# First loads of a two-layer trunk in a pool of their own, adaLN products in 256 columns, the dt projection beside B and C

## The chip, the cores and the metric

The kernel runs on one core of a Trainium2 chip (trn2). The metric is the device time of one execution in microseconds; runs of a kernel differ by about 0.2%.

## The reference, cut to what matters

Two layers over 512 latent tokens and 256 context tokens of width 1024, all in float32. Only the start of a layer matters here: the adaLN shift and scale of the two conditioning vectors, the modulated RMS norm, and the first columns of one combined projection, which feed the SSD scan.

```
shift, scale, gate = jnp.split(jax.nn.silu(c) @ w_ada + b_ada, 3, axis=-1)
...
h  = rms_norm(x) * (1.0 + scale[:, None]) + shift[:, None]
hc = rms_norm(xc) * (1.0 + scale_c) + shift_c
...
p = h @ w_in
xbc, dt_raw, k, v, u, uv, g_a, z, q, g_c = jnp.split(p, _cuts(CTX_SIZES + LAT_SIZES), axis=-1)
...
xh, bm, cm, dts = ssd_prepare(xbc, dt_raw, conv_w, conv_b, dt_bias)
ys, _, _ = ssd_bidir(xh, bm, cm, dts, a_neg, hf_c, hb_c, True)
```

`ssd_prepare` convolves the columns of x, B and C and turns `dt_raw` into step sizes; the scan needs cumulative sums of these.

## The kernel before, in words

Activations lie feature-major in SBUF: 8 feature blocks (k = 0 to 7) of 128 rows by 768 tokens, 256 of context first. Each product of float32 factors is made of three passes: every factor is split in a high part and a rest (`h_hi`, `h_lo`; `whi`, `wlo`), and high by high, rest by high and high by rest are accumulated in one PSUM bank. A bank holds 512 columns, so a projected block of 128 columns takes two banks, one of 512 columns (latents, `fl`) and one of 256 (context, `fcx`).

The order on each engine is made by a scheduler that simulates the program when it is built, and takes what is ready by priority (`tc.high_priority`); on the chip each engine runs its instructions in that order. Tiles with the same tag share a few buffers, and a writer waits for the last reader of its buffer.

Layer 0 begins in `first_layer_in`. The SP queue issues the loads: the conditioning vectors `cc`, the weights of B and C (`rawb`, `rawc`, 512 KB each), six token tiles `xn` of 512 KB (L257), then w_ada in 16 tiles `wa` of 128 columns (L265, 512 KB, rows of 512 bytes), which share four buffers with the tag `Fb`. ACT, POOL and DVE normalize the token tiles (Square L288, power L141 and L142, scaling L290). For each feature block k, `ada_in(k)` makes the shift and scale: 16 narrow products `pa` of 128 columns (L270), a copy `part` to SBUF by ACT (L272), two products with `sel` that sum the four partial rows (L274), and `mod` by DVE (L275). It is called two blocks ahead (`NAH = 2`). Then the normalized tiles are transposed by PE into `pt` (L297), DVE applies `mod` while reading the bank (`hf`, L299), ACT makes `h_hi` (L145), DVE makes `h_lo` (L146), and PE multiplies the block into the four open banks of B and C, three passes each (L305 to L307).

The dt projection, 32 columns as a two-part weight `wst`, is written behind it as two accumulations of 16 products (`accdt`, L496 to L499), copied to `dtf` by ACT (L500). Then come the convolutions (ACT copies the banks to `xp`, L450 and L451, DVE adds the taps, L456) and the next projected blocks (`proj`, the products `accc`, L387, L391, L392). A block's weights need one of two buffers `whi`: ACT writes it (`whic`, L145), then DVE its rest (`wloc`, L146). From `dtf` a chain of small steps leads to cumulative sums, which POOL writes to memory (`csd`, L551) and reads back spread over the partitions (`Fb`, L601); DVE and ACT make the scan's decay factors of it (L605, L608).

```
def ada_in(k):
    with tc.high_priority((HPW0, HPW1, HPW)[min(k, 2)] if FL else HPW):
        wa = [sp.tile([P, KD, P], F32, tag="Fb", bufs=4, name=f"wa0_{k}_{i}") for i in range(2)]
...
for k in range(NAH):
    ada_in(k)
```

Of the kernel before, what the change touches and what calls it, by code (L numbers as in the profile page):

```python
# [11 lines left out]
F32 = mybir.dt.float32  # L12
F32R = mybir.dt.float32r
# [31 lines left out]
NAH = 2  # L45
HPX = 20000
HPS = 20000
HPW = 9000
# [5 lines left out]
DTB = "sc"  # L54
TKD = -1
FL = 0
HPW0 = 50000
HPW1 = 14000
HPC = 12000
# [3 lines left out]
LAG = 1  # L63
# [28 lines left out]
def tile_hybrid_trunk(ctx: ExitStack, tc: tile.TileContext, ins, out: bass.AP):  # L92
# [59 lines left out]
    def params(li):  # L152
# [3 lines left out]
        with tc.high_priority(0 if li or not FL else 8 * HP):  # L156
            nc.sync.dma_start(prm, ins["prm"][li])
        L.b_ada = prm[:, 0:24]
# [27 lines left out]
    def ada_steps(mp, todo):  # L186
        """todo: (layer, its index, first of four blocks); one step for each block"""
# [63 lines left out]
    def first_layer_in(L, sp, sx, ws, w_split):  # L251
        """norm and modulation of the inputs by feature blocks, the first projections beside it"""
        xn = [sx.tile([P, 3, DM], F32, tag="xT", bufs=2, name=f"xn{i}") for i in range(2)]
        rs = small.tile([P, TT, 2], F32, tag="rs0", bufs=1, name="rs0")
        for t in (2, 3, 4, 5, 0, 1) if FL else range(TT):
            with tc.high_priority(HPC if FL and t < 2 else HPX):
                nc.sync.dma_start(xn[t // 3][:, t % 3, :], x_rows(0, t))  # L257

        def ada_in(k):
            """shift and scale of feature block k"""  # L260
            with tc.high_priority((HPW0, HPW1, HPW)[min(k, 2)] if FL else HPW):
                wa = [sp.tile([P, KD, P], F32, tag="Fb", bufs=4, name=f"wa0_{k}_{i}") for i in range(2)]
                for i in range(2):
                    c0 = DM * i + P * k
                    nc.sync.dma_start(wa[i], ins["w_ada"][0, :, c0 : c0 + P].rearrange("(k p) m -> p k m", p=P))  # L265
            pa = bank("sc", f"pa0_{k}")
            for i in range(2):
                for q in range(KD):
                    j = q % 4
                    pe.matmul(pa[32 * j : 32 * j + 32, P * i : P * i + P], sc[:, q, :], wa[i][:, q, :], start=q < 4, stop=q >= 4)  # L270
            part = small.tile([P, 2, P], F32, tag="part0", name=f"part0_{k}")
            act.activation(part, pa[:, 0:256].rearrange("p (i m) -> p i m", i=2), AF.Copy)  # L272
            for i in range(2):
                pe.matmul(pa[:, 256 + 2 * i : 258 + 2 * i], part[:, i, :], sel, start=True, stop=True)  # L274
                dve.tensor_scalar(  # L275
                    L.mod[:, 8 * i + k, :], pa[:, 256 + 2 * i : 258 + 2 * i], L.b_ada[:, 8 * i + k : 8 * i + k + 1], float(i), ALU.add, ALU.add
                )

        lat = [bank("acc", f"fl{i}") for i in range(2)]
        cx = [bank("sc", f"fcx{i}") for i in range(2)]  # L280
        for k in range(NAH):
            ada_in(k)
        with tc.high_priority(HPS):
            hl = [w_split(c0, name) for c0, name in ws]
        if not FL:
            for t in range(TT):
                xt = xn[t // 3][:, t % 3, :]
                act.activation(h_lo[:, 6:8, 0:512], xt.rearrange("p (a b) -> p a b", a=2), AF.Square, accum_out=rs[:, t, 0:1])  # L288
                rstd_pow(rs[:, t, 1:2], rs[:, t, 0:1], 1.0 / DM, EPS)
                dve.tensor_scalar(xt, xt, rs[:, t, 1:2], None, ALU.mult)  # L290
            for k in range(KD):
                hf32 = t3(f"hf0_{k}")
                for s, (o, n) in enumerate(SEGS):
                    pt = bank("at", f"pt0_{k}_{s}")
                    for i in range(n // P):
                        t = o // P + i
                        pe.transpose(pt[:, P * i : P * i + P], xn[t // 3][:, t % 3, P * k : P * k + P], ident)  # L297
# [5 lines left out]
                for i, (hi, lo) in enumerate(hl):  # L303
                    for acc, sl in ((cx[i][:, :NCX], slice(0, NCX)), (lat[i], slice(NCX, NT))):
                        pe.matmul(acc, hi[:, k, :], h_hi[:, k, sl], start=k == 0, stop=False)  # L305
                        pe.matmul(acc, hi[:, k, :], h_lo[:, k, sl], start=False, stop=False)
                        pe.matmul(acc, lo[:, k, :], h_hi[:, k, sl], start=False, stop=k == KD - 1)  # L307
        else:
# [819 lines left out]
```

## Time and profile before

| what | value |
|---|---|
| time, median of 3 runs | 1448.0 us (1446.86 to 1449.85) |
| profiled execution, first to last instruction | 1448.3 us |
| PE busy | 1337.9 us, 92% |
| DVE busy | 945.3 us, 65% |
| ACT busy | 656.1 us, 45% |
| POOL busy | 214.5 us, 15% |
| mean granted TensorE clock | 0.964 |

The profile gives the profiled execution as its span; no other time of that execution is listed beside it, and it lies within the three runs. PE is busy in nearly the whole span, so what matters is where it stands idle and where it runs at less than its full clock; both are read from tables of short stretches and from the engines' timelines. PE is TensorE, DVE VectorE, ACT ScalarE, POOL GpSimd, SP the queue of SyncE; L12 is line 12.

### The profile page before, as it was taken

Reading aid. Unit: us, or ns where it says so; the run is one execution under the profiler, and the core shown is the slowest. Engines: PE = TensorE matmul, PEld = TensorE weight load, DVE = VectorE, ACT = ScalarE, POOL = GpSimd, SP = SyncE. Lnnn points to the kernel's source line nnn. Section 1 sums busy time; section 2 is a strip of 40 time slices with the busy share of each in tenths; the row PEclk is TensorE's granted clock in tenths of the full one; section 3 lists DMA queues with packets and bytes.
Section 4 is the critical chain, followed back from the end, with each engine's and each line's share of the span. In section 5 each row is a group of like instructions: output and inputs, shape, how many; then the busy total and the mean of one; then the engine's idle time right before and its main releaser. Section 6 shows DMA issues by size and latency. Waiting matters only on the chain.

```text
span 1448.3 us, 21208 instructions
## 1 busy us (share of the span) xinstructions
PE 1337.9 (92%) x7944; PEld 1101.8 (76%) x7944; DVE 945.3 (65%) x1465; ACT 656.1 (45%) x1406; POOL 214.5 (15%) x418
## 2 busy tenths in 40 slices
PE   4999999999988999999999989999999689989987
PEld 3787888778867787788887768778778557778765
DVE  4497897587576657775232458887677477787432
ACT  3257634624455547554121235833623455575320
POOL 2002023113101113220000000202213001222000
PEclk8999999999999989999999999999999899989999
DMA  9424255745937447567878522625737954557885
GB/s 290 125 74 131 72 164 169 204 127 189 310 112 200 138 138 237 168 202 255 249 236 238 160 67 64 161 84 164 219 102 205 255 155 127 188 161 231 267 270 162
DMA packets 271782, 255.97 MB, mean 177 GB/s; under 512 B 14384, under 2 KB 223552, under 8 KB 271680
## 3 DMA queue, kind: packets, MB, share of 16 engines
q1 hardware_dynamic: 176624, 126.07, 31.1%
q0 software_dynamic: 18800, 66.68, 14.7%
q10 hardware_dynamic: 76256, 61.88, 13.9%
q8 instruction: 62, 1.02, 0.3%
q14 instruction: 40, 0.33, 0.1%
HBM read 199.12 MB, written 49.17 MB: 171 GB/s over the span
## 4 chain that ended last, share of the span: by engine, by line
PE 53%; DMA 18%; issue 12%; DVE 9%; ACT 6%; POOL 2%; SPq 1%; ACTq 0%; DVEq 0%; POOLq 0%
PE oacc L1027 4%; PE oacc L1026 4%; PE oacc L1025 4%; DMA Fb<-csd 3%; DMA yl<-ydr 3%; DMA qsq<-kq 2%; PE pS L585 2%; PE accc L387 2%; PE accc L391 2%; PE accc L392 2%; ACT Fb L608 2%; PE pO L790 2%; DMA qsk<-kq 2%; PE po L640 2%; PE acck L387 2%
## 5 line engine op out<-in xcount | busy, mean ns | idle before, releaser
L608 ACT ACTIVATE Fb<-Fb,dt_fp 128x128 f32<-128x128 f32 x320 | 98.6, 392 | 89.2 <-DVE Fb L605 89.2
L387 PE MATMUL accc<-h_hi,whic 128*128 128x512 f32 (+1 forms) x312 | 108.5, 348 | 5.5 <-ACT xp L451 3.8
L391 PE MATMUL accc<-h_lo,whic 128*128 128x512 f32 (+1 forms) x312 | 107.2, 344 | 0.0
L392 PE MATMUL accc<-h_hi,wloc 128*128 128x512 f32 (+1 forms) x312 | 106.8, 342 | 0.3 <-DVE wloc L146 0.3
L1025 PE MATMUL oacc<-wohi,yl 128*128 128x512 f32 x240 | 95.1, 396 | 5.0 <-DMA yl<-ydr 3.9
L1027 PE MATMUL oacc<-wohi,yl 128*128 128x512 f32 x240 | 95.4, 397 | 2.8 <-DMA yl<-ydr 2.8
L456 DVE SCALAR_TENSOR_TENSOR yv<-xp,hal,yv 128x772 f32<-128x772 f32 (+1 forms) x96 | 94.1, 993 | 5.7 <-ACT yv L454 4.5
L1026 PE MATMUL oacc<-wolo,yl 128*128 128x512 f32 x240 | 94.8, 395 | 1.0 <-DVE wolo L146 1.0
L756 ACT ACTIVATE Ea<-sm,mx 128x768 f32<-128x768 f32 (+1 forms) x80 | 65.2, 816 | 47.9 <-DVE mx L754 34.7
L605 DVE TENSOR_TENSOR Fb<-Fb,dt_cs 128x1024 f32<-128x1024 f32 x40 | 48.8, 1221 | 50.1 <-DMA Fb<-csd 50.0
L754 DVE TENSOR_REDUCE mx<-sm 128x1 f32<-128x768 f32 (+1 forms) x80 | 67.1, 843 | 13.6 <-PE sm L752 13.5
L387 PE MATMUL accz<-h_hi,whiz 128*128 128x512 f32 (+1 forms) x192 | 71.9, 375 | 0.8 <-DVE gtz L426 0.4
L391 PE MATMUL accz<-h_lo,whiz 128*128 128x512 f32 (+1 forms) x192 | 70.3, 366 | 0.0
L392 PE MATMUL accz<-h_hi,wloz 128*128 128x512 f32 (+1 forms) x192 | 70.1, 365 | 0.0
L387 PEld LDWEIGHTS accc<-h_hi,whic 128*128 128x128 f32 x312 | 59.4, 190 | 13.9 <-ACT xp L451 5.1
L749 PE MATMUL sm<-kh,qq 128*128 128x256 f32 (+1 forms) x144 | 52.5, 382 | 14.6 <-ACT Ea L756 12.9
L790 PE MATMUL pO<-v,wt 128*128 128x128 f32 x416 | 59.4, 295 | 6.5 <-DVE gg L801 4.8
L637 POOL DMA_DIRECT2D EF<-ecd x72 | 44.7, 627 | 139.3 <-DVE xT L642 128.3
L392 PEld LDWEIGHTS accc<-h_hi,wloc 128*128 128x128 f32 x312 | 59.5, 191 | 7.3 <-DVE wloc L146 0.5
L391 PEld LDWEIGHTS accc<-h_lo,whic 128*128 128x128 f32 x312 | 59.4, 190 | 6.8 <-issue 0.7
L790 PEld LDWEIGHTS pO<-v,wt 128*128 128x128 f32 x416 | 55.2, 207 | 11.6 <-DVE gg L801 5.5
L1043 DVE TENSOR_TENSOR go<-oacc,gate 128x512 f32<-128x512 f32 x20 | 13.7, 687 | 70.9 <-PE oacc L1027 70.9
(374 smaller groups left out, 3874.5 us busy)
## 6 DMA issues: line engine op xcount, KB each, us to landing
yl<-ydr ACTq DMA_DIRECT2D x120, 256.0 KB
wa<-in_w_ada SPq DMA_DIRECT2D x48, 512.0 KB
Fb<-csd POOLq DMA_DIRECT2D x40, 512.0 KB, 5.9
wo<-in_w_out SPq DMA_DIRECT2D x32, 512.0 KB
rawc<-in_w_in SPq DMA_DIRECT2D x22, 512.0 KB
EF<-ecd POOLq DMA_DIRECT2D x72, 128.0 KB, 3.1
rawz<-in_w_in SPq DMA_DIRECT2D x16, 512.0 KB
ydr<-yhi ACTq DMA_DIRECT2D x12, 384.0 KB
```

The costliest lines, as they stand in the source:

```text
L387: m = pe.matmul(acc[:, :n], hi[:, k, :], h_hi[:, k, o : o + n], start=k == 0, stop=False)
L391: pe.matmul(acc[:, :n], hi[:, k, :], h_lo[:, k, o : o + n], start=False, stop=False)
L392: pe.matmul(acc[:, :n], lo[:, k, :], h_hi[:, k, o : o + n], start=False, stop=k == KD - 1)
L456: dve.scalar_tensor_tensor(yv[:, lo_:], xp[:, lo_ + tap : tap + W2], L.convh[:, j, tap : tap + 1], yv[:, lo_:], ALU.mult, ALU.add)
L608: act.activation(Fb[:, h, :], Fb[:, h, :], AF.Exp, bias=fp[:, o : o + 1])
L749: m = pe.matmul(c_, H.qs[i][:, tsl], H.kh[i][:, k0 : k0 + kn], start=True, stop=False)
L754: dve.tensor_reduce(mx[:, i : i + 1], smap[:, s0 : s0 + nk], AX.X, ALU.min)
L756: act.activation(Es[i], smap[:, s0 : s0 + nk], AF.Exp, bias=mx[:, i : i + 1], scale=-1.0, accum_out=z[:, i, t % 2 : t % 2 + 1])
L790: pe.matmul(o_, H.w[:, k, P * ql : P * ql + P], H.v[:, k, :], start=k == 0, stop=k == nkt - 1)
L1025: pe.matmul(accs[t], yh[0][:, k, :], whi, start=q == 0 and k == 0, stop=False)
L1026: pe.matmul(accs[t], yh[0][:, k, :], wlo, start=False, stop=False)
L1027: pe.matmul(accs[t], yh[1][:, k, :], whi, start=False, stop=q == 3 and k == 3)
```

## The change

1. Layer 0's first loads go to a pool `start` that is open only while `first_layer_in` runs, and the scan's pools open after it in the same space. It holds the six token tiles and all of the shift and scale columns of w_ada, as eight tiles `wa` of 256 columns (1 MB each, rows of 1 KB). So no `wa` waits for a buffer. The token tiles are requested on the ACT queue, latents first; `wa` stays on SP; `prm` goes to the POOL queue.
2. `ada_in(q)` makes two feature blocks at once: 16 products of 256 columns (L277), one copy of 512 columns (L279), four products with `sel` into a second bank `pm` (L282), and two DVE operations for `mod` (L285). It is written just before the two blocks that need it. Banks of `pa`, `pm` and `pt` share the tag `at`, which has two buffers; `pa` had the tag `sc`.
3. The dt projection runs inside the loop over k: four more products for each k into two more banks of the tag `sc` (`fldt`, `fcdt`, L300 to L303). Its copies `dtf` are L324 and L325. Within a block the latents now come before the context.

The later program is written as before.

```diff
-        def ada_in(k):
-            with tc.high_priority((HPW0, HPW1, HPW)[min(k, 2)] if FL else HPW):
-                wa = [sp.tile([P, KD, P], F32, tag="Fb", bufs=4, name=f"wa0_{k}_{i}") for i in range(2)]
...
-            pa = bank("sc", f"pa0_{k}")
...
-        for k in range(NAH):
-            ada_in(k)
...
-                if k + NAH < KD:
-                    ada_in(k + NAH)
...
+        with tc.tile_pool(name="start", bufs=1, reuse_waits="tile") as su:
+            xn = [su.tile([P, DM], F32, name=f"xn{t}") for t in range(TT)]
...
+                    wa[q, i] = su.tile([P, KD, 256], F32, name=f"wa0_{q}_{i}")
+                    c0 = DM * i + 256 * q
+                    nc.sync.dma_start(wa[q, i], ins["w_ada"][0, :, c0 : c0 + 256].rearrange("(k p) m -> p k m", p=P))
+
+            with tc.high_priority(HPS0):
+                for t in (2, 3, 4, 5, 0, 1):
+                    nc.scalar.dma_start(xn[t], x_rows(0, t))
+                load_ada(0)
+                blocks, wst = weights()
+                for q in range(1, 4):
+                    load_ada(q)
...
+            def ada_in(q):
+
+                pa = bank("at", f"pa0_{q}")
+                for i in range(2):
+                    for k in range(KD):
+                        j = k % 4
+                        pe.matmul(pa[32 * j : 32 * j + 32, 256 * i : 256 * i + 256], sc[:, k, :], wa[q, i][:, k, :], start=k < 4, stop=k >= 4)
+                part = su.tile([P, 4, P], F32, tag="part0", bufs=2, name=f"part0_{q}")
+                act.activation(part, pa.rearrange("p (i m) -> p i m", m=P), AF.Copy)
+                pm = bank("at", f"pm0_{q}")
+                for i in range(4):
+                    pe.matmul(pm[:, 2 * i : 2 * i + 2], part[:, i, :], sel, start=True, stop=True)
...
+            ldt, cdt = bank("sc", "fldt"), bank("sc", "fcdt")
+
+            def dt_part(acc, k, sl):
+                if k == KD - 1:
+                    pe.matmul(acc[:32], wst[:, k, 0:32], h_lo[:, k, sl], start=False, stop=False)
+                pe.matmul(acc[:64], wst[:, k, :], h_hi[:, k, sl], start=k == 0, stop=k == KD - 1)
+                if k < KD - 1:
+                    pe.matmul(acc[:32], wst[:, k, 0:32], h_lo[:, k, sl], start=False, stop=False)
+
             for k in range(KD):
+                if k % 2 == 0:
+                    ada_in(k // 2)
...
+                for acc, adt, sl in ((lat, ldt, slice(NCX, NT)), (cx, cdt[:, :NCX], slice(0, NCX))):
...
+                    dt_part(adt, k, sl)
+            dtf = t3("dtf0")
+            act.activation(dtf[:64, NCX:], ldt[:64], AF.Copy)
+            act.activation(dtf[:64, :NCX], cdt[:64, :NCX], AF.Copy)
```

**Where the order changes: PE between two feature blocks.** Before, at the step from k = 4 to k = 5 (`pa_6` and `pa_5` are the adaLN products of feature blocks 6 and 5, `pt_5` the transposed block 5, `fl` and `fcx` the products of B and C):

```order
L307 MATMUL fl_150<-h_hi,wloc_0_216 128x512
L270 MATMUL pa_6_466<-wa_6_1_463,sc 32x128 x8
L297 MATMUL pt_5_0_504<-ident,xn_140 128x128 x2
L297 MATMUL pt_5_1_508<-ident,xn_140 128x128
L274 MATMUL pa_5_414<-sel,part_5_431 128x2
L305 MATMUL fcx_151<-h_hi,whib_0_209 128x256
L305 MATMUL fl_149<-h_hi,whib_0_209 128x512
```

Now, at the step from k = 1 to k = 2 (`pa_1` and `pm_1` belong to blocks 2 and 3, `pa_2` to blocks 4 and 5; four more rows of `pt` like those shown stand in the gap marked):

```order
L303 MATMUL fcdt<-h_lo,wst_134 32x256
L277 MATMUL pa_1_297<-wa_1_1_172,sc 32x256 x2
L282 MATMUL pm_1_316<-sel,part_1_314 128x2 x4
L313 MATMUL pt_2_1_324<-ident,xn_140 128x128
...
L313 MATMUL pt_2_0_330<-ident,xn_138 128x128
...
L313 MATMUL pt_3_1_353<-ident,xn_140 128x128
...
L319 MATMUL fl_207<-h_hi,whib_0_156 128x512
L319 MATMUL fl_208<-h_hi,whic_0_162 128x512
L301 MATMUL fldt<-h_hi,wst_134 64x512
...
L277 MATMUL pa_2_381<-wa_2_0_174,sc 32x256 x8
```

Before, the shift and scale of block 6 were in work while block 4 was multiplied, and what stood between two blocks had been prepared. Now 14 of the 16 adaLN products of a pair stand among the products of the pair before it, the last two directly ahead of it, and the sums `pm`, all twelve transposes of the pair and its first product stand behind them in one row. At the step from k = 3 to 4 it is the same with three products; at the step from 5 to 6 all 16 stand in block 4, and the row begins with `pm`.

**ACT at the end of the stage.** Before (`xp` are copies of the banks for the convolution, `whic` the high parts of the weights of the next two blocks, `dtf` the copy of dt):

```order
L145 ACTIVATE h_hi<-hf_7_580 128x768
L450 ACTIVATE xp_8_607<-fcx_151 128x256
L145 ACTIVATE whic_0_741<-rawc_0_739 128x1024
L451 ACTIVATE xp_8_607<-fl_149 128x512
L145 ACTIVATE whic_1_812<-rawc_1_810 128x1024
```

Now:

```order
L136 ACTIVATE h_hi<-hf_7_520 128x768
L324 ACTIVATE dtf_549<-fldt 64x512
L452 ACTIVATE xp_8_561<-fl_207 128x512
L136 ACTIVATE whic_0_653<-rawc_0_651 128x1024
L451 ACTIVATE xp_8_561<-fcx_209 128x256
L136 ACTIVATE whic_1_724<-rawc_1_722 128x1024
L325 ACTIVATE dtf_549<-fcdt 64x256
```

The weights of the next block, which stood behind one copy of 256 columns, stand behind two copies of 512. The copies of dt, which came after both convolutions' first steps, now come ahead of them or among them.

## Rows read from the trace of the kernel before

**Rows 1.** Stretches (us from the start): busy time of each engine (instructions), granted clock, DMA share, GB/s.

```profile
25.00:30.00 5.00, 3.83 (x13) 3.16 (x14) 3.92 (x17) 1.56 (x4) 0.00 (x0) 0.61 1.15 287
45.00:50.00 5.00, 5.00 (x30) 3.63 (x29) 1.39 (x3) 0.84 (x1) 0.00 (x0) 0.50 0.72 179
50.00:74.00 24.00, 23.95 (x216) 18.98 (x212) 12.05 (x21) 6.64 (x11) 0.34 (x6) 1.00 0.16 44
74.00:120.00 46.00, 45.73 (x271) 40.14 (x271) 41.78 (x66) 23.88 (x36) 0.68 (x12) 1.00 0.26 70
120.00:146.00 26.00, 23.31 (x145) 20.13 (x144) 18.70 (x21) 20.70 (x54) 9.51 (x21) 0.93 0.61 172
...
851.00:853.00 2.00, 0.36 (x3) 0.36 (x3) 2.00 (x7) 0.89 (x2) 0.17 (x3) 1.00 0.00 0
```

**Rows 2.** The same view, two stretches of the first loads.

```profile
7.50:12.50 5.00, 0.00 (x0) 0.00 (x0) 1.62 (x2) 1.57 (x2) 0.00 (x0) 1.00 1.03 405
...
20.00:45.00 25.00, 22.31 (x218) 15.85 (x211) 12.53 (x42) 5.42 (x13) 1.24 (x5) 0.76 1.20 283
```

**Rows 3.** Timeline of the SP queue: start, us, engine, line, operation, tiles, count.

```profile
6.08 11.42 SPq L265 DMA_DIRECT2D wa<-in_w_ada  x4
...
33.07 18.40 SPq L265 DMA_DIRECT2D wa<-in_w_ada  x8
```

**Rows 4.** Timeline of PE, first half of the stage; in brackets idle time and releaser.

```profile
19.47 1.08 PE L270 MATMUL pa<-wa,sc 128*32 128x128 f32 x16
...
27.81 0.77 PE L305 MATMUL fl<-h_hi,whib 128*128 128x512 f32 x1
...
42.73 0.67 PE L270 MATMUL pa<-wa,sc 128*32 128x128 f32 x16 [0.63 <-DMA wa<-in_w_ada]
...
48.09 0.63 PE L306 MATMUL fl<-h_lo,whic 128*128 128x512 f32 x1
48.51 0.63 PE L307 MATMUL fl<-h_hi,wloc 128*128 128x512 f32 x1
```

**Rows 5.** Timeline of PE, second half of the stage.

```profile
50.97 0.87 PE L297 MATMUL pt<-ident,xn 128*128 128x128 f32 x6
...
57.33 0.39 PE L306 MATMUL fl<-h_lo,whib 128*128 128x512 f32 x1
57.56 0.40 PE L307 MATMUL fl<-h_hi,wlob 128*128 128x512 f32 x1
```

**Rows 6.** Groups of instructions between 18 and 76 us: count, busy us, mean ns, idle before.

```profile
L145 ACT ACTIVATE h_hi<-hf 128x768 fp32r<-128x768 f32 x8 | 6.8, 845 | 18.2 <-DVE hf L299 18.2
L299 DVE TENSOR_SCALAR hf<-pt,mod 128x512 f32<-128x512 f32 x8 | 6.4, 803 | 0.5 <-PE pt L297 0.3
L274 PE MATMUL pa<-sel,part 128*128 128x2 f32 x32 | 5.6, 246 | 0.4 <-ACT part L272 0.4
L299 DVE TENSOR_SCALAR hf<-pt,mod 128x256 f32<-128x256 f32 x8 | 4.3, 541 | 0.2
...
L275 DVE TENSOR_SCALAR mod<-pa,prm 128x2 f32<-128x2 f32 x16 | 3.5, 217 | 18.7 <-PE pa L274 18.7
...
L146 DVE TENSOR_TENSOR wloc<-rawc,whic 128x1024 fp32r<-128x1024 f32 x2 | 2.5, 1226 | 3.4 <-ACT whic L145 3.4
```

**Rows 7.** Timeline of PE at the end of the stage.

```profile
73.42 0.28 PE L499 MATMUL accdt<-h_hi,wst 128*64 128x256 f32 x1
...
74.53 0.39 PE L392 MATMUL accc<-h_hi,wloc 128*128 128x256 f32 x1 [0.28 <-DVE wloc L146]
```

**Rows 8.** Timeline of ACT at the end of the stage.

```profile
72.17 1.05 ACT L145 ACTIVATE whic<-rawc 128x1024 fp32r<-128x1024 f32 x1
73.12 0.59 ACT L451 ACTIVATE xp<-fl 128x512 f32<-128x512 f32 x1
```

**Rows 9.** Timeline of PE where the scan's first factors are made.

```profile
134.46 0.50 PE L387 MATMUL accc<-h_hi,whic 128*128 128x512 f32 x1 [2.04 <-ACT xp L451]
```

**Rows 10.** Timeline of POOL in the same place.

```profile
122.72 3.57 POOL L601 DMA_DIRECT2D Fb<-csd  x4 [1.63 <-DMA csd<-cse]
```

More of the change, by code (lines that the diff above doesn't have):

```diff
@@ L44 @@
 NWP = 2
[L45 to L48, printed above, removed]
+HPS0 = 60000
 NPART = 2
@@ L62 @@
 HPV = 0
-LAG = 1
 NADA = (2, 1)
@@ L155, in params @@
         prm = small.tile([P, 24 + 12 * 6 + 21], F32, tag="prm", name=f"prm{li}")
-        with tc.high_priority(0 if li or not FL else 8 * HP):
+        if li:
             nc.sync.dma_start(prm, ins["prm"][li])
+        else:
+            with tc.high_priority(HPS0):
+                nc.gpsimd.dma_start(prm, ins["prm"][li])
         L.b_ada = prm[:, 0:24]
@@ L339, in first_layer_in @@
-        return [(cx[i][:, :NCX], lat[i]) for i in range(2)]
+                for acc, adt, sl in ((lat, ldt, slice(NCX, NT)), (cx, cdt[:, :NCX], slice(0, NCX))):
+                    for i, (hi, lo) in enumerate(blocks):
+                        pe.matmul(acc[i], hi[:, k, :], h_hi[:, k, sl], start=k == 0, stop=False)
+                        pe.matmul(acc[i], hi[:, k, :], h_lo[:, k, sl], start=False, stop=False)
+                        pe.matmul(acc[i], lo[:, k, :], h_hi[:, k, sl], start=False, stop=k == KD - 1)
+                    dt_part(adt, k, sl)
@@ L341, in tile_hybrid_trunk @@
+            dtf = t3("dtf0")
+            act.activation(dtf[:64, NCX:], ldt[:64], AF.Copy)
+            act.activation(dtf[:64, :NCX], cdt[:64, :NCX], AF.Copy)
+        return [(cx[i], lat[i]) for i in range(2)], dtf
     with tc.high_priority(HPR):
@@ L435, in finish, with dt_weights @@
             Q["yl"].dma_start(ydr[1, kt, :, tl0:], lo[:, tl0:].bitcast(F32))
-        with tc.tile_pool(name=f"ssd{li}", bufs=1, reuse_waits="tile") as sp, tc.tile_pool(name=f"ssx{li}", bufs=1, reuse_waits="tile") as sx, tc.tile_pool(name=f"ps_s{li}", bufs=3, space=PSUM, reuse_waits="tile") as ps2:
+        with ExitStack() as sstack:
+            ps2 = sstack.enter_context(tc.tile_pool(name=f"ps_s{li}", bufs=3, space=PSUM, reuse_waits="tile"))
+            def dt_weights(wst):
+                raw = load_w(C_DT, 32, f"dt{li}")
+                split(wst[:, :, 0:32], wst[:, :, 32:64], raw[:, :, 0:32])
+                return wst
+            if li == 0:
+                wst = gen.tile([P, KD, 64], F32R, name="wst0")
+                first, dtf = first_layer_in(
+                    L, bank, lambda: ([w_split(C_B, "b0_0"), w_split(C_C, "c0_0")], dt_weights(wst))
+                )
+            sp = sstack.enter_context(tc.tile_pool(name=f"ssd{li}", bufs=1, reuse_waits="tile"))
+            sx = sstack.enter_context(tc.tile_pool(name=f"ssx{li}", bufs=1, reuse_waits="tile"))
             W = TT * 32
@@ L481, in tile_hybrid_trunk @@
             if li == 0:
-                bc_blocks(0, first_layer_in(L, sp, sx, [(C_B, "b0_0"), (C_C, "c0_0")], w_split))
+                bc_blocks(0, first)
             else:
```

121 lines of the change are left out of this document (36 added, 85 removed).

## Prediction

> **What bounds the kernel now.** I read the table of short stretches first, because the page's shares (PE 92%) average over stages with different limits. The change touches one stage, from the first load to the end of the dt projection at 73.7 us [rows 7], so the question is what ends last there, and whether a delay gets through to the end afterwards. The stretches answer the second part: from 74 to 120 us PE is busy for 45.73 of 46 us at a granted clock of 1.00, with DVE at 41.78 [rows 1]. There is no slack that could swallow a shift, so what the stage loses or gains goes nearly one to one into the time, except where a later wait of PE becomes shorter.
>
> The stage has three parts. Up to 19.47 us loads bound it: the first adaLN product starts when its first tile is there, and the first product of B and C follows at 27.81 [rows 4], that is 8.3 us later. Then, to about 50 us, PE is busy but slow: the granted clock is 0.61 from 25 to 30 us and 0.50 from 45 to 50 [rows 1] (0.50 is the level of 1.2 GHz, 1.00 that of 2.4). The second fall came behind some microseconds of light work, adaLN products that used 32 columns of the array and an idle wait of 0.63 us for a load [rows 4]. Two products of 512 columns follow each other after 0.42 us there [rows 4] and after 0.23 us at the full level [rows 5]. From 50 us to the end PE is busy for 23.95 of 24 us at 1.00 [rows 1]: the two-block look-ahead keeps it fed.
>
> **The loads.** In the change 6.6 MB have to land before the first adaLN product can end: B and C 1.05, six token tiles 3.15, a pair of `wa` 2.1, and 0.25 of small ones. Token tiles (rows of 4 KB) moved at 405 GB/s, rows of 512 bytes at 283 [rows 2]. For rows of 1 KB nothing is shown; between the two I take 350. That gives 3.7 + 7.8 + 6.0 = 17.5 us; with the two rates put to `wa`, 16.7 to 18.9. The same sum for before, with half as much `wa` at 283, is 3.7 + 7.8 + 3.7 = 15.2 us against 19.47 measured, so 4.3 us are start and what shares the lines. Some of that sharing goes (the second pair comes behind the first), so I put the first adaLN products at 21.0, between 20 and 23. The Trainium skill (DMA: Bandwidth & Descriptors, Specifications) gives 512 B as the least transfer for line rate; by it 1 KB rows bring nothing over 512 B, and the sum would be 1.4 us longer. The trace disagrees as far as it goes, with 283 against 405 GB/s.
>
> That all loads are requested at once matters little after this. Before, the queue was held for 11.42 us over four `wa` and 18.40 over eight [rows 3], partly for buffers, but the lines were at 283 GB/s from 20 to 45 us anyway [rows 2]: 2.1 MB of a further pair need 6 to 7.4 us, and PE needs a pair only every 11 us. So I cost the three later pairs at nothing. The `prm` and `row` loads move too, and nothing early waits for them but `mod`, which comes after.
>
> From the first adaLN product to the first product of B and C I keep 8.3 us [rows 4]: the products are 16 of 256 columns (1.8 to 3.4 us by clock) for 32 of 128, and the copy, sum, `hf`, `h_hi` are the same steps in a row. First product of B and C: 29.3, 1.5 later than before.
>
> **The loop, at full clock.** For each k there are 12 products of B and C and 4 of dt, half of 512 columns (0.23 us [rows 5]) and half of 256 (half of it): 8 x 0.23 + 8 x 0.115 = 2.76 us, 5.5 for a pair. The dt products cost before what they cost now, only elsewhere. The adaLN products of a pair are 16 x 0.115 = 1.8 us, as before. What is new stands between the pairs. With no look-ahead for `pm`, and with two buffers for `pa`, `pm` and `pt`, this is a chain: copy `part` of 512 columns (0.59, as the ACT copy of 512 columns of a bank [rows 8]), four sums (0.5: 0.25 each by the group, two overlapping [rows 6]), two `mod` (2 x 0.22), `hf` (0.80 + 0.54), `h_hi` (0.85) [rows 6], and about 0.4 of hops: 4.1 us. In it PE does only the sums and twelve transposes, 12/6 x 0.87 = 1.7 us [rows 5]; it idles for about 1.9. Pairs start 5.5 + 1.8 + 4.1 = 11.4 us apart, the last of them 10.8, since there the copy is done ahead. Stage end: 29.3 + 11.4 + 11.4 + 10.8 + 5.5 = 68.4, 5.3 us earlier than 73.7. That gain is all from the slow clock before.
>
> **The clock.** I don't think it goes away. The first pair again starts behind light work; before, the first 8 us of B and C ran at the lower level, which cost about half of that. I take +3.5 (0 to +4.5). Then each of the three gaps has 4 us with sums and transposes alone and nearly 2 us of idle PE. For a fall: the light stretch ahead of 45 us, which was followed by 5 us at 0.50, at a cost of 2.5 or a little more [rows 1, 4]; and the wait of 2.04 us before 134.46 [rows 9], in a stretch whose clock is 0.93 [rows 1]. Against: from 851 to 853 us PE was busy for 0.36 of 2 us, and the clock in it stayed 1.00 [rows 1]. So each gap costs 0 to 3 us; I take 1.7, nearer to the fall because two cases speak for it, 5.1 in all. Stage end: 68.4 + 3.5 + 5.1 = 77.0, **+3.3**. With no fall 68.4 (-5.3), with all of them 81.9 (+8.2).
>
> **The hand-over.** Before, the next block's weights were being written while PE did the last dt products, and PE waited 0.28 us for `wloc` [rows 7]. Now dt ends with the rest, so those products no longer cover anything, and ACT does two copies of 512 columns (0.59 each) before `whic` (1.05 [rows 8]); behind it DVE makes `wloc` (1.23 [rows 6]). That is 3.5 us from the last use of B's weights, of which PE can fill about 0.6 with what is left of C and dt, and some with the passes that need no `wloc`. Taken: **+2.2** (1 to 3). Queued behind on ACT is the second `whic`, needed a block later: nothing.
>
> **Later.** With `dtf` copied first, the chain to `csd` starts earlier against the products, and the read of `Fb` at 122.72 [rows 10] with it. Of PE's 2.04 us at 134.46 and the lower clock around it (26 us at 0.93, about 1.8) [rows 1, 9] at most 3.8 can come back; I take **-1.5**. Later waits may be reshuffled a little; I give them no sign.
>
> **Sum.** +3.3 + 2.2 - 1.5 = +4.0 on the profiled execution's 1448.3, so 1452.3; that execution is 0.3 over the median of the runs, well inside their spread, so I round to 1452.5.
>
> **Rivals.**
> Faster: *PE keeps its full clock*. The loads come in one go, the first pair is dense (32 products and the adaLN of the next), and the gaps are short enough. Then the stage ends 5.3 us earlier, and -5.3 + 2.2 - 1.5 to -3.8 gives 1441.5 to 1443.7. For it: the 1.00 at 851 us. Against it: both falls in the stage before. It decides where the clock costs under 1.7 us in all four places together (under 4 if all of the late wait comes back).
> Unchanged: *gains and losses cancel*. The first pair is slow, the gaps are not: -5.3 + 3.5 + 2.2 - 1.5 = -1.1, 1447; one fall of 2.5 more makes 1449.7. It is the case between.
> Not what it says: *the loads aren't the limit that went*. If the first adaLN product waits for the whole 6.6 MB at 283 GB/s, the first pair starts 2 us later, and the later pairs still wait for nothing; 1454.5, inside my own case.
> Slower by more: every gap falls, +8.2 + 2.2 - 1.5 = +8.9, 1457; without the late gain 1459.
>
> **How the numbers follow.** My forecast with its slower neighbours (a fall at two or three gaps) has 0.52, and its own range is 1451 to 1460. The case between has 0.26 and the full clock 0.22. The range of 1442.5 to 1460 leaves out the ends of both sides. A difference of 0.2% (2.9 us) is about what can be told from no change: faster is under 1445.1, slower over 1450.9. The bounds fall between the cases, so the chances are 0.23, 0.25 and 0.52.
>
> **What would show it.** First product of B and C near 29 us; gaps of nearly 2 us of PE idle behind `pm`, each with a granted clock of 0.5 to 0.9 behind it; end of the stage near 77; the first `wloc` wait grown to 2 us; the wait before the first decay factors shorter than 2.04. The forecast is wrong if the clock stays at 1.00 from 30 us on, or if PE doesn't idle between pairs because the scheduler's order lets the transposes and `hf` of the second block cover it.

## The result, and the profile after

| | median | runs | ratio to before |
|---|---|---|---|
| changed | 1471.6 us | 1464.47 to 1477.69 (4) | 1.0158 [1.0120, 1.0196] |
| before, beside it | 1448.9 us | 1446.86 to 1452.98 (4) | |
| changed once more (e4) | 1469.5 us | 1462.33 to 1475.56 (6) | 1.0139 [1.0105, 1.0174] |

The change makes the kernel 20 to 23 us slower. I had forecast 1452.5 us and a range up to 1460: the sign was right, the size was not. The profiled execution has a span of 1475.9 us and took 1477.69 us, the most of the four, so what is read from its profile adds up to more than the medians lost.

PE's timeline of the changed kernel: the first products, the first gap between two pairs of blocks (in full) and the first product behind each of the other two, the hand-over to the next block (`accc`), and three later places. The rows answer to [rows 4, 5, 7, 9]:

```profile
20.15 1.94 PE L277 MATMUL pa<-wa,sc 128*32 128x256 f32 x16 [20.15 <-DVE sc L122]
...
30.12 0.80 PE L319 MATMUL fl<-h_hi,whib 128*128 128x512 f32 x1
30.71 0.63 PE L319 MATMUL fl<-h_hi,whic 128*128 128x512 f32 x1
31.14 0.56 PE L301 MATMUL fldt<-h_hi,wst 128*64 128x512 f32 x1
...
40.64 1.05 PE L282 MATMUL pm<-sel,part 128*128 128x2 f32 x8 [0.70 <-ACT part L279]
41.55 0.96 PE L313 MATMUL pt<-ident,xn 128*128 128x128 f32 x6
43.09 0.89 PE L313 MATMUL pt<-ident,xn 128*128 128x128 f32 x6 [0.58 <-DVE hf L315]
44.42 0.50 PE L319 MATMUL fl<-h_hi,whib 128*128 128x512 f32 x1 [0.44 <-ACT h_hi L136]
44.76 0.40 PE L319 MATMUL fl<-h_hi,whic 128*128 128x512 f32 x1
44.99 0.40 PE L301 MATMUL fldt<-h_hi,wst 128*64 128x512 f32 x1
...
57.45 0.50 PE L319 MATMUL fl<-h_hi,whib 128*128 128x512 f32 x1 [0.44 <-ACT h_hi L136]
...
68.89 0.50 PE L319 MATMUL fl<-h_hi,whib 128*128 128x512 f32 x1 [0.44 <-ACT h_hi L136]
...
74.98 0.28 PE L301 MATMUL fcdt<-h_hi,wst 128*64 128x256 f32 x1
76.73 0.38 PE L374 MATMUL accc<-h_hi,whic 128*128 128x256 f32 x1 [1.47 <-ACT whic L136]
...
77.99 0.39 PE L379 MATMUL accc<-h_hi,wloc 128*128 128x256 f32 x1 [0.76 <-DVE wloc L137]
...
143.03 0.50 PE L374 MATMUL accc<-h_hi,whic 128*128 128x512 f32 x1 [1.63 <-ACT xp L452]
...
397.65 1.54 PE L728 MATMUL pvt<-ident,vf 128*128 128x128 f32 x6 [3.55 <-DMA vf<-vd]
...
431.84 0.69 PE L776 MATMUL ptw<-ident,Ea 128*128 128x128 f32 x2 [5.49 <-DVE Ea L771]
```

The gap is there as forecast: PE waits for `part`, for `hf` and for `h_hi`, 1.72 us in all. The last dt product ends at 75.3 us, 1.6 later than [rows 7]. Then PE waits 2.23 us for the next block's weights, against 0.28 before. ACT's timeline shows why: the copy of dt and a copy of a bank come ahead of `whic` (before, [rows 8], `whic` was being made while PE did the dt products):

```profile
74.66 0.59 ACT L324 ACTIVATE dtf<-fldt 64x512 f32<-64x512 f32 x1 [4.26 <-PE fldt L301]
75.15 0.58 ACT L452 ACTIVATE xp<-fl 128x512 f32<-128x512 f32 x1
75.63 1.05 ACT L136 ACTIVATE whic<-rawc 128x1024 fp32r<-128x1024 f32 x1
```

The stretches, with the columns of [rows 1], show what follows that wait:

```profile
20.00:40.00 20.00, 18.53 (x116) 11.38 (x116) 8.02 (x15) 5.46 (x11) 3.94 (x8) 1.00 1.11 334
32.00:38.00 6.00, 6.00 (x48) 3.87 (x48) 1.03 (x2) 0.84 (x1) 0.00 (x0) 1.00 1.09 349
40.00:50.00 10.00, 8.35 (x65) 5.99 (x66) 6.85 (x26) 2.92 (x7) 0.17 (x3) 1.00 0.79 207
50.00:74.00 24.00, 20.96 (x150) 15.41 (x149) 9.15 (x16) 4.58 (x6) 0.34 (x6) 1.00 0.00 1
75.00:80.00 5.00, 2.77 (x19) 2.32 (x18) 3.29 (x3) 4.92 (x10) 0.00 (x0) 0.93 0.13 31
80.00:84.00 4.00, 4.00 (x19) 3.75 (x18) 3.96 (x6) 0.95 (x1) 0.00 (x0) 0.50 0.80 225
84.00:88.00 4.00, 4.00 (x12) 3.29 (x12) 4.00 (x9) 1.48 (x3) 0.17 (x3) 0.50 0.02 4
88.00:120.00 32.00, 32.00 (x183) 28.02 (x182) 25.11 (x44) 15.15 (x22) 0.51 (x9) 0.98 0.18 50
...
120.00:146.00 26.00, 23.63 (x142) 20.70 (x141) 21.14 (x24) 20.63 (x50) 7.92 (x17) 1.00 0.63 150
```

In this execution the clock stays at 1.00 through all three gaps and falls to 0.50 (the level of 1.2 GHz) from 80 to 88 us, behind the hand-over's wait: 8 us at half speed, 4 lost, and about 1 more by the rows on either side (0.93 and 0.98). So the scan's first blocks of products begin 7.6 to 9.8 us later than before, and the lag is still 10.4 us at the scan's end (367 us before). The rest comes later. The last two of PE's rows above lie in the first layer's attention, and behind the second stands this row of DVE's timeline:

```profile
430.36 0.69 DVE L688 TENSOR_TENSOR qsq<-qsq,sin 128x512 f32<-128x512 f32 x1 [4.16 <-DMA qsq<-kq]
```

Neither place was touched by the change, and before PE has neither wait. The lag against before is 19 us at the first MLP block (577.9 us before), 15 at the start of the second layer and 27.6 at the last output product. So three questions: what the start costs and which of its edits does it, why more is lost behind the scan, and how my sum stands to both.

### The profile page after: what moved, and what is told of

Same layout as the page of the kernel before. It is cut to its first block, busy times and chain, and to the rows that moved or that the text cites. A ratio compares the mean times of both kernels' runs of the same rounds, so it can differ in the third digit from the quotient of the medians.

```text
span 1475.9 us, 20899 instructions
## 1 busy us (share of the span) xinstructions
PE 1343.4 (91%) x7816; PEld 1103.5 (75%) x7816; DVE 942.9 (64%) x1457; ACT 657.2 (45%) x1402; POOL 217.3 (15%) x419
## 3 DMA queue, kind: packets, MB, share of 16 engines
q10 hardware_dynamic: 77120, 65.03, 14.3%
## 4 chain that ended last, share of the span: by engine, by line
PE 54%; DMA 22%; DVE 10%; issue 7%; ACT 5%; POOL 1%; ACTq 0%; SPq 0%; DVEq 0%; POOLq 0%
DMA Fb<-csd 4%; PE oacc L1026 3%; PE oacc L1024 3%; PE oacc L1025 3%; DMA qsq<-kq 3%; PE accc L374 2%; PE accc L378 2%; PE accc L379 2%; PE pO L789 2%; PE pS L584 2%; DMA yl<-ydr 2%; PE po L639 2%; DMA qsk<-kq 2%; DMA wo<-in_w_out 1%; PE accz L374 1%
## 5 line engine op out<-in xcount | busy, mean ns | idle before, releaser
L607 ACT ACTIVATE Fb<-Fb,dt_fp 128x128 f32<-128x128 f32 x320 | 98.7, 392 | 71.7 <-DVE Fb L604 71.7
L137 DVE TENSOR_TENSOR wolo<-wo,wohi 128x1024 fp32r<-128x1024 f32 x32 | 38.7, 1223 | 39.0 <-ACT wohi L136 39.0
```

The costliest lines, as they stand in the source:

```text
L607: act.activation(Fb[:, h, :], Fb[:, h, :], AF.Exp, bias=fp[:, o : o + 1])
```

## The experiments

In all of them the program computes the same as before. A ratio is against runs of the kernel before on the same chip; 0.1% is 1.4 us. The kernel before spread wider there than the 0.2% that I had started from: 1443.2 to 1453.6 us in eleven runs beside e1 to e4. Lags are starts of the same block of products, minus those of the profile before; the scan's first block is its first of 512 columns, at 77.26 us before.

That profile is one execution. All nine profiles that keep its later order (e1, e3, e5, e6, e9 and e12 to e15) gain 3 to 5 us on it between 475 and 600 us and lose 5 to 11 between 1150 and 1291 us, whatever their start. So a lag tells of a change as far as the scan's end; behind it the ratios count, and two profiles of the study against each other.

### The start, and the order of what comes later (e1, e2, e4)

The scheduler orders the whole program again when its start changes. Behind dt both kernels issue the same 10043 instructions, but 2660 of PE's 6534 stand in another place, and 651 of DVE's 1388. A table at the end of the kernel can hold those instructions to either order, by dependences that order two instructions on an engine and add no semaphore.

```diff
         tile_hybrid_trunk(tc, ins, out)
+        keep_order(tc)
...
+            if e in last:
+                tc.add_manual_dep(i, last[e].name, NOSYNC, reason="order of the table")
+            last[e] = i
```

e1 is the changed kernel with the later order of before, e2 the kernel before with the later order of the changed one, e4 the changed kernel as it is.

> The start of the changed kernel, and behind the dt projection the instructions of every engine in the order that they had in the kernel before (a table holds the order; nothing is computed otherwise). Theory L, most of the loss is in the later order that the scheduler made anew: only the start's part stays, the 7.6 to 10 us that separate the profiles from 85 to 390 us, so 1456 to 1459 and 1.005 to 1.007 of before. Theory S, the start alone costs it, and its delay makes the later transfers come at worse times: 1468 to 1474, ratio 1.013 to 1.018. In its profile the later waits of PE tell which: 3.5 us for vf and 5.5 us for Ea near 400 and 432 us should be gone by theory L.

> The start of the kernel before, and behind the dt projection the order of the changed kernel. Theory L: it loses what the later order costs, 10 to 14 us, 1459 to 1463. Theory S: the order costs nothing by itself, 1447 to 1451.

> The changed kernel itself, timed again on the same chip as the three others, since its four runs lie 13 us apart. Both theories: 1464 to 1478, median near 1471, ratio 1.012 to 1.019. If it comes out under 1460 the first result was partly chance.

Measured: e1 1.0100 [1.0066, 1.0133], e2 1.0094 [1.0058, 1.0131], e4 1.0139 [1.0105, 1.0174]. Both halves cost. On the old start the new order alone costs 14 us, well clear of the intervals; on the new start (e4 against e1) it is about 5.7, the size of the intervals. The two halves overlap. The profile of e4, the changed kernel's fastest run (1462.33 us), has a lag of 9.9 us at the scan's end and 12.3 at the end, where the first profile had 10.4 and 27.6. e1's lag is 8.6 us at the scan's first block and 7.8 at its end, with falls of the clock now at two of the three gaps, as I had forecast for each (44 to 48 and 58 to 62 us), and a smaller one behind the hand-over:

```profile
44.00:48.00 4.00, 3.37 (x14) 2.33 (x14) 3.45 (x7) 1.74 (x3) 0.00 (x0) 0.66 0.81 227
58.00:62.00 4.00, 3.43 (x14) 2.62 (x13) 3.09 (x5) 1.38 (x2) 0.00 (x0) 0.61 0.02 4
80.00:84.00 4.00, 2.70 (x16) 2.50 (x17) 3.44 (x4) 3.92 (x8) 0.00 (x0) 0.85 0.22 56
84.00:88.00 4.00, 4.00 (x19) 3.62 (x19) 4.00 (x5) 1.15 (x2) 0.00 (x0) 0.72 0.76 212
```

So which gap falls differs between executions: over six profiles of this start the stage ends at 75.3, 76.4, 77.4, 78.1, 78.4 and 79.1 us. Over four of the old start (before, e2, e7, e8) it ends at 73.7, 73.2, 71.7 and 71.4: the profile that every lag here is taken from is the latest of them.

### Which part of the order (e7, e8)

The old start, with the first layer's scan in the old order and the rest in the new one (e7), or the other way round (e8).

```diff
-    for text in (ORDER0, ):
+    for text in (ORDER0, ORDER1, ):
```

> The start of the kernel before; behind it the first layer's scan in the order of before, and from the attention of the first layer on the order of the changed kernel. The second run (all of the later order new) lost 14 us, of which its profile shows 9 in the scan. Theory L1, all of that loss is in the scan, where the dt chain was moved ahead: 1448 to 1452. Theory L2, the later parts cost as much as they seem to in the profile: 1454 to 1458.

> The counterpart: the start of the kernel before, the first layer's scan in the order of the changed kernel, the rest in the order of before. Theory L1: 1460 to 1464, PE waits 1.2 us for dtf near 78 us with a granted clock under 0.8 behind it. Theory L2: 1455 to 1459.

Measured: e7 1.0034 [1.0016, 1.0052], e8 1.0036 [1.0015, 1.0056]. No single place holds the loss. In e8's profile PE waits 1.19 us for the copy `dtf` at 75.97 and the clock is 0.84 and 0.82 in the next two stretches of 5 us; e7 has no such wait.

### The hand-over alone (e3)

e1, with the copies of dt behind the first steps of the convolutions and `whic` first on ACT.

```diff
-            act.activation(dtf[:64, NCX:], ldt[:64], AF.Copy)
-            act.activation(dtf[:64, :NCX], cdt[:64, :NCX], AF.Copy)
-        return [(cx[i], lat[i]) for i in range(2)], dtf
+        return [(cx[i], lat[i]) for i in range(2)], (ldt, cdt)
...
+                dtf = t3("dtf0")
+                act.activation(dtf[:64, NCX:], ldt[:64], AF.Copy)
+                act.activation(dtf[:64, :NCX], cdt[:64, :NCX], AF.Copy)
```

> The kernel of the first run of this study, with two changes at the end of the first stage: the copies of dt come after the first steps of both convolutions, and the next block's weights are the first thing that ACT does once B's weights are free. If the hand-over and the low clock behind it make up most of what the start lost, PE's idle time between the last dt product and the third product of the next block falls from 2.2 us to about 1.2, the granted clock of 79 to 86 us rises from about 0.5 to 1.00, and the time falls by 4 to 6 us against the first run. If the clock falls all the same: by 1 us only.

Measured: 1.0106 [1.0076, 1.0135], e1's ratio. The waits for `whic` and `wloc` fall from 1.47 and 0.76 us to 1.05 and 0.27, and the clock behind them holds, as PE's timeline and the stretches of e3 show:

```profile
79.15 0.39 PE L371 MATMUL accc<-h_hi,whic 128*128 128x256 f32 x1 [1.05 <-ACT xp L449]
...
79.92 0.39 PE L376 MATMUL accc<-h_hi,wloc 128*128 128x256 f32 x1 [0.27 <-DVE wloc L137]
```

```profile
80.00:84.00 4.00, 4.00 (x28) 3.78 (x29) 3.62 (x4) 3.91 (x8) 0.00 (x0) 1.00 0.69 180
84.00:88.00 4.00, 4.00 (x19) 3.19 (x17) 4.00 (x5) 0.81 (x2) 0.00 (x0) 1.00 0.30 88
```

The lag at the scan's first block falls to 5.4 us from 8.6, and the time does not move. In the two profiles e3's lag is below e1's up to 688 us (3.8 against 6.7), level with it at 866 (5.5 against 5.7) and above it from 942 on (8.7 against 6.4): what the hand-over gave is lost again, in these two at the change of layers and in the second layer's scan. Why it is lost, no run shows.

### The places of the scan's buffers (e5, e11)

The first tile with a tag decides where its buffers lie. Before, `wa` was the first `Fb`, and the scan's first tile; now `bT` comes first. In the changed kernel and in e1 the load `wsT` for the attention then lands in space that the scan still reads, and POOL holds it, and the queue behind it, for `py` (8.57 us in the changed kernel's profile). POOL's timeline of e1:

```profile
373.70 0.56 POOL L867 DMA_DIRECT2D wsT<-in_wsT  x1 [4.62 <-PE py L620]
```

e5 is e1 with two tiles that nothing uses, which put the buffers where they were. e11 does the same in the changed kernel, with the scheduler free.

```diff
+                sp.tile([P, 8, P], F32, tag="Fb", bufs=4, name="fb_first")
                 bc_blocks(0, first)
+                sp.tile([P, KD, 64], F32R, tag="H0", bufs=NHF, name="h0_first")
```

> The first run of this study (new start, later order of the kernel before), and the scan's pool gives its tiles the places that they had before: two tiles that nothing uses are allocated where the loads had stood, so that Fb lies at the pool's start again. In the first run POOL's loads for the attention (wsT) waited 4.6 us for a product that reads Fb, and PE waited 3.3 us for vf behind it, which it did not with the old start. Theory M, the shift of places is the cause: both waits fall under 1 us, and the time falls by 2 to 4 us against the first run, to 1459 to 1461. If the waits stay, the later burst of loads has another cause and the time stays near 1463.

> The changed kernel with two unused tiles at the head of the scan's pools, so that the scan's buffers lie where they did before; the scheduler is free. Theory 1, the places cost 3 to 5 us in the changed kernel as they did between e1 and e5: ratio 1.010 to 1.013, and the attention of the first layer without the 3 us wait for its load. Theory 2, the scheduler makes yet another order from the same edits and the places' gain is lost or doubled by it: a ratio outside 1.008 to 1.014, with the wait for the load gone all the same.

Measured: e5 1.0068 [1.0044, 1.0091], e11 1.0093 [1.0061, 1.0126]. POOL's timeline of e5 shows the load without a wait, and PE's the row that had waited 3.28 us in e1:

```profile
367.12 0.56 POOL L869 DMA_DIRECT2D wsT<-in_wsT  x1
```

```profile
390.03 0.87 PE L730 MATMUL pvt<-ident,vf 128*128 128x128 f32 x6 [0.23 <-DMA vf<-vd]
```

The places cost about 4.6 us (e1 against e5), and 6.7 in e11 against e4, where the order was made anew as well. The differences are of the size of the intervals, so the cost in time is likely and not shown; the wait itself is gone in both profiles.

### The loads and the 256 columns alone (e6, e9, e12)

e5 with dt behind B and C again and `pa`, `pm` in the banks `sc`, one pair ahead. (Four banks `sc` hold B's and C's context products and either dt or the look-ahead, so in these banks the one excludes the other; e14 below finds room for the look-ahead in `at`.)

```diff
-                pa = bank("at", f"pa0_{q}")
+                pa = bank("sc", f"pa0_{q}")
...
+            ada_in(0)
             for k in range(KD):
-                if k % 2 == 0:
-                    ada_in(k // 2)
...
+                if k % 2 == 0 and k < 6:
+                    ada_in(k // 2 + 1)
...
-                    dt_part(adt, k, sl)
```

> Of the change only the loads and the products of 256 columns: the adaLN products of a pair are called one pair ahead, in the banks that the dt products had taken, and dt is projected after B and C as before; places and later order are those of the run with the scan's map as before. Theory G, the lost look-ahead and the dt products in its place make the gaps, the hand-over wait and the low clock behind them: the first product of B and C starts at 29 to 30 us, no gap of over 0.7 us from there, the stage ends at 64 to 68 us (73.7 before, 75 to 79 changed), and the time is 1441 to 1446, faster than before. Theory K, the loads themselves make the start late or the clock falls whatever stands between the pairs: stage end 72 or later, and 1449 or more.

Measured: 0.9987 [0.9966, 1.0007], and letter for letter once more (e12) 0.9984 [0.9956, 1.0011].

> e6 once more, letter for letter. If the loads and the 256 columns alone are worth the 2 us that e6's ratio of 0.9987 suggests: 0.997 to 1.000 again, the stage at the start again ahead of the kernel before by 4 to 5 us. If e6 was luck: 1.000 to 1.003.

The loss of the changed start is gone. PE's timeline and a stretch of e6 show no gap up to the last dt product, which ends at 67.7 us, 6.0 ahead of [rows 7]; behind it PE waits 0.76 us for `wloc`.

```profile
33.16 0.48 PE L311 MATMUL fl<-h_hi,whib 128*128 128x512 f32 x1
...
67.38 0.28 PE L490 MATMUL accdt<-h_hi,wst 128*64 128x256 f32 x1
...
69.02 0.39 PE L367 MATMUL accc<-h_hi,wloc 128*128 128x256 f32 x1 [0.76 <-DVE wloc L137]
```

```profile
50.00:68.00 18.00, 17.90 (x116) 14.38 (x115) 7.41 (x15) 5.20 (x9) 0.17 (x3) 1.00 0.00 0
```

Of a lead of 5.5 us in the scan the medians keep about 2. e12's profile is ahead by 2 to 9 us until the second layer's attention and level from 1291 us on, where all these profiles lose against the one before; e6's is still 8.1 ahead at the end.

The first product of B and C came late there, at 33.16. ACT stands still for 5.08 us until `rawc` lands and can split it; behind it in its queue are four tiles' squares and the gate of `cc`. e9 orders these by hand ahead of it.

```diff
-HAND = ()
+HAND = (('I-183', 'I-93', 'I-187', 'I-191', 'I-195', 'I-199', 'I-203', 'I-164', 'I-229'),
...
```

(The first row is ACT's: the squares and, second, the gate's tanh, then C's split, I-164, and the first `part`.)

> The loads and the 256 columns alone, with dt behind B and C, as in e6, and with an order by hand on three engines: ScalarE squares all six input tiles and takes the gate's tanh ahead of C's weight split, VectorE follows it, and TensorE takes the first block's transposes ahead of the second pair's adaLN product; at the end of the stage the hand-over's first weight split comes first on ScalarE. In e6 the first projection began at 33.16 us and waited for the scaling of the input's tiles, while the stage ended at 67.7 us. Theory 1, the late squares are what e6 still loses of the loads: first projection at 29 to 30 us, the stage's end at 64 to 66 us, 1 to 3 us faster than e6 (ratio 0.996 to 0.998). Theory 2, TensorE's own work or a fall of its granted clock behind the earlier start fills the gain: first projection at 29 to 30 us, the stage's end at 67 to 68 us, the time as e6.

Measured: 0.9986 [0.9961, 1.0010], as e6. The first product is at 30.39 and the last dt product ends at 68.9, 1.3 later than in e6: theory 2. Its early products of 512 columns are 0.42 us apart (32.69 and 33.11), where e6's, which come later, are 0.24 apart (34.22 and 34.46), and PE's own work fills the rest. The late first product costs nothing.

### e6 without the table (e10)

```diff
-        keep_order(tc)
```

> e6's edits without the table that holds the later program to the order of the kernel before: the scheduler is free to place what stands behind dt. Theory 1, a new order of the later program costs by itself, whatever the start: 3 to 7 us slower than e6 (1452 to 1457 us, ratio 1.002 to 1.006), with a stage at the start as in e6. Theory 2, the order costs only in the company of the changed kernel's hand-over: as e6, 1447 to 1450 us.

Measured: 1.0273 [1.0230, 1.0315], the largest effect of the study and far outside what I expected: the same edits, and 41 us more, by the order alone. Its start is e6's (lag -4.7 us at the first block). The lag is +20 us at the first MLP block and +41.3 at the last output product. One of the places, in the timelines of PE, ACT, POOL and DVE, each released by the next:

```profile
527.08 0.47 PE L790 MATMUL pO<-ident,osq 128*128 128x128 f32 x1 [5.77 <-ACT osq L789]
```

```profile
526.66 0.37 ACT L789 ACTIVATE osq<-pO,r 128x128 f32<-128x128 f32 x1 [5.61 <-POOL r L787]
```

```profile
525.92 0.71 POOL L787 TENSOR_TENSOR r<-r,mhalf 128x2 f32<-128x2 f32 x1 [17.61 <-DVE r L786]
```

```profile
524.01 0.69 DVE L680 TENSOR_TENSOR qsq<-qsq,sin 128x512 f32<-128x512 f32 x1 [4.25 <-DMA qsq<-kq]
...
525.61 0.15 DVE L786 SCALAR_TENSOR_TENSOR r<-ss,r 128x2 f32<-128x2 f32 x1
```

DVE stands at a rotation whose load `qsq` isn't there yet, and 0.15 us of work on `r` is queued behind it. Through POOL and ACT this holds PE for 5.77 us. It is the row that stood at 430.36 in the changed kernel, with `Ea` behind it and PE idle for 5.49. Before, DVE waits for such a load too (2.83 us at 423.81), with `Ea` behind it, but PE has other products to do there and does not stand still.

### Look-ahead or dt beside (e13, e14, e15)

Between e6 and e5 are two edits, and these runs separate them. e13 is e6 without the look-ahead (`pa`, `pm` in the banks `at`, before their blocks). e14 is e5 with it: dt beside B and C, and PE's order in the stage by hand, so that `pa` stands behind the first block of the pair before, `pm` and the next transposes among the products of its second. e15 is e14 with B's products first in the last block and `whic` ahead of the copies of dt. The edit shown is e14's, against e5.

```diff
+            ada_in(0)
             for k in range(KD):
-                if k % 2 == 0:
-                    ada_in(k // 2)
...
+                if k % 2 and k < 7:
+                    ada_in(k // 2 + 1)
```

> e6 with one thing taken away, the look-ahead: the adaLN products go to the banks of the transposes and are written just before their two blocks, as in the changed kernel; dt stays behind B and C, places and later order as before. Theory 1, the lost look-ahead makes the cost of the changed start: TensorE's idle gaps return at three of the pairs of blocks, the last product of the stage ends at 73 to 77 us (67.7 in e6), without a wait for the copies of dt behind it; ratio 1.003 to 1.006. Theory 2, dt beside and its hand-over make the cost: the time as e6, 0.997 to 1.000.

> e5 with dt still beside B and C, and the look-ahead given back within the two banks of the transposes: TensorE's order is set by hand so that a pair's adaLN products stand behind the first block of the pair before, their sums and the next transposes among the products of its second block. Theory 1, the lost look-ahead: hardly an idle gap between 31 us and the stage's end, which comes at 69 to 72 us (77 to 78 in e5); the hand-over's wait of 2 us stays; ratio 1.000 to 1.003. Theory 2, dt beside and its hand-over: gaps gone and the time still as e5, 1.005 to 1.008.

> e14, and in the last block the products with B's weight come first, so that its buffer is free early; ScalarE makes the next block's weight split first, then the copies of dt and of the context. Theory 1, the hand-over's wait is on the path: no wait over 0.5 us between the last product of the stage and the next block, granted clock 1.00 from 75 to 90 us, 2 to 5 us faster than e14 (0.997 to 1.001). Theory 2, as in e3, what the hand-over gives is lost again later: wait gone, time as e14 within 0.3%.

| | look-ahead | dt | last product ends | lag at the scan's first block | ratio |
|---|---|---|---|---|---|
| e6 | yes | behind | 67.7 us | -5.5 us | 0.9987 [0.9966, 1.0007] |
| e13 | no | behind | 71.2 us | -2.0 us | 1.0030 [1.0005, 1.0055] |
| e14 | yes | beside | 72.8 us | +0.7 us | 1.0019 [1.0000, 1.0037] |
| e15 | yes | beside, no hand-over wait | 74.6 us | +0.1 us | 1.0019 [0.9997, 1.0040] |
| e5 | no | beside | 77.4 us | +7.1 us | 1.0068 [1.0044, 1.0091] |

Both theories hold, each for half. The look-ahead is worth 0.0043 and 0.0049, 6 to 7 us, whichever way dt goes, and dt beside costs 0.0032 and 0.0038, about 5; the second pair is only just clear of its intervals. PE at the boundary between two pairs, e13 and then e14:

```profile
54.00 0.50 PE L310 MATMUL fl<-h_hi,whib 128*128 128x512 f32 x1 [0.44 <-ACT h_hi L136]
```

```profile
52.83 0.50 PE L320 MATMUL fl<-h_hi,whib 128*128 128x512 f32 x1 [0.93 <-ACT h_hi L136]
```

In e13 this boundary costs 0.44 us of idle time although nothing is computed ahead (the changed profile idled for 1.72): the scheduler has put dt products of the block before ahead of the sums and between the transposes. That is what dt behind B and C was good for. Its products were the filling for the gaps, and at the end the cover for the hand-over. Written into the loop they come when B and C come, and fill nothing. e15's wait at the hand-over is gone (no row over 0.5 us), its clock is 0.66 from 70 to 75 us, ahead of the hand-over, and the time is e14's, as in e3.

## Why the prediction was wrong

**What bounds it** held: the stage's loss reaches the scan one to one, and there is no slack from 74 to 120 us.

**The loads** held in size. First adaLN product at 20.15 us (forecast 21.0), first of B and C at 30.12 (29.3). The reason was another in part: the first adaLN product waited for `sc`, whose ACT step stood behind the split of `rawc`. It cost nothing. In e4, the same kernel, `sc` came 3.4 us earlier, but the pair's second `wa` tile landed when it did in the first profile (22.38), and the first product of B and C was at 30.01. PE's timeline of e4:

```profile
16.73 1.93 PE L277 MATMUL pa<-wa,sc 128*32 128x256 f32 x16 [16.73 <-DVE sc L122]
22.27 1.94 PE L277 MATMUL pa<-wa,sc 128*32 128x256 f32 x16 [3.61 <-DMA wa<-in_w_ada]
```

Rows of 1 KB moved at 349 GB/s from 32 to 38 us, where I had put 350 (334 over 20 to 40); [rows 2] had 283 for 512 bytes. The Trainium skill (DMA: Bandwidth & Descriptors, Specifications) gives 512 B as the least transfer for line rate. By it the rows of all three loads would move alike; they disagree, with 283, 349 and 405 GB/s for 512 B, 1 KB and 4 KB. Not having to wait for `wa` is worth something after all where PE can use it: e6 ends the stage 6.0 us earlier than the profile before, 3.7 earlier than the earliest of the old start.

**The loop** came out right by two errors that cancel. At full clock I had 39.1 us from the first product of B and C to the end. The changed profile, with no fall of the clock behind any gap, has 45.1: pairs start 14.3, 13.0 and 11.4 us apart and the last takes 6.4, where I had 11.4, 11.4, 10.8 and 5.5. The gap itself is close (1.72 us idle, forecast 1.9). But a pair's adaLN products took 1.9 us where they stood together and 2.5 to 3.0 where the scheduler had parted them (forecast 1.8). The step from the last adaLN product to the next pair's first product took 4.5 (forecast 4.1): the four sums are eight rows in the trace and took 0.91, where I had read 0.5 from [rows 6]. The clock I had charged 8.6 us. It cost that execution less than 1 us before 79 us, in its first products (0.43 us apart), and others, with a fall at one or two of the gaps, some 3 us there (e1's 0.66 and 0.61 over 4 us each). Stage end forecast 77.0, measured 75.3 to 79.1.

**The hand-over** was right as a wait, +2.2 us forecast, 2.23 measured against 0.28, so 1.95 more. I priced no fall of the clock behind it, though I had priced one behind each gap: that made 4 to 5 us in the changed profile (0.50 from 80 to 88 us). Whether this term counts in the time is less clear: without the wait neither e3 nor e15 was faster.

**Later** is the step that failed: "Later waits may be reshuffled a little; I give them no sign", and -1.5 us in all. Of the gain the profile shows something where I looked for it: a wait of 1.63 us at 143.03 in place of the 2.04 of [rows 9], and a clock of 1.00 from 120 to 146 us in place of 0.93. It does not show in the lag, which is 10.4 us at the scan's end. What I had left without a price was far larger: the new order of the later program cost 14 us on the old start (e2) and some 5.7 on this one (e4 against e1), and the places of the scan's buffers some 4.6 (e1 against e5); the last two are the size of their intervals, the first is clear of them. The text of the later program is the same and I had taken that for the same program. I had compared the orders up to the hand-over and read no further.

**The sum.** Forecast: start +5.5, later -1.5. Measured: start +9.9 (e5; 6.4 to 13.2 by its interval), places +4.6, order +5.7. These are the steps from before to e5, e1 and e4, so that they add up to e4's 20.1 is no check; the first measurement had 22.9. My 5.5 for the start lies just under e5's interval, so how much it was too small is open: e5's lag at the scan's first block is 7.1, that of the changed profile up to 9.8, both against the latest of the old start's profiles.

**The rivals.** "PE keeps its full clock" came true in one execution from 31 to 79 us and gave no gain, since the loop at full clock was itself 5 to 6 us longer. No rival had the later program in it. The rival of the loads had a slip: 6.6 MB at 283 GB/s are 23.3 us, 6 more than my 17.5 and not 2; it did not come about. That the transposes and `hf` could cover the gap was named as what would make me wrong; the scheduler did not do it, and the look-ahead set by hand is worth 7 us (e14 against e5).

No version clearly beats the kernel before: e6, e9 and e12 lie at 0.9984 to 0.9987, some 2 us faster, each with 1.0 inside its interval.

## What to carry to other kernels

Where a scheduler places the instructions, an edit at the start is an edit of the whole program: hold the rest to its old order and its buffers to their old places before you judge the edit, for here the order alone was worth some 6 to 41 us (e4 against e1, e10 against e6) and the edits 2 to 10. Independent work written behind a loop is filling for the loop's gaps and cover for what follows; look for what it fills before you fold it in. And where two things want the same banks (here dt and the look-ahead), price what the one takes from the other; e14 had both, in the banks of the transposes.

## What the runs showed of the hardware

- The granted clock in the stretches reads 1.00 from 20 us on in the changed profile, but products of 512 columns follow each other after 0.43 us at the start (30.71 and 31.14) and after 0.23 later (44.76 and 44.99). At the start a 1.00 there was not the full speed.
- The same waits are followed by different falls of the clock from one execution to the next. The first two gaps between pairs gave none in the changed profile, with 1.72 and 1.79 us of idle PE, and 0.66 and 0.61 over 4 us each in e1's; 2.23 us of wait at the hand-over gave 8 us at 0.50 in the one, and 0.85 and 0.72 over 4 us each in the other.
- DVE, waiting 4.25 us for a load, held what was queued behind it in e10, and that came out as 5.77 us of idle PE three engines on.
